# Three modulation slices summed on VectorE, and a longer pad ahead of the expert tiles, in a hybrid retention and mixture-of-experts layer

## The chip, the cores and the metric

One core of a Trainium2 chip runs the whole layer in one launch. The metric is the device time of an execution in microseconds; the time before is the median of three timed runs.

## The reference, cut to what matters

One layer over 2048 tokens of width 1024, in float32, with 256 context tokens and 16 experts. The modulation is one row vector, cut into six slices of 1024 numbers:

```python
mod = jax.nn.silu(c) @ w_ada[l] + b_ada[l]
sh1, sc1, g1, sh2, sc2, g2 = jnp.split(mod[:, None, :], 6, axis=-1)
h = modulate(x, sh1, sc1)                      # _ln(x) * (1 + sc1) + sh1
y = token_mixer(h @ w_in[l], ...)              # conv, retention, gates
x = layer_norm(DEEPNORM_ALPHA * x + g1 * y, ln1_g[l], ln1_b[l])
h = modulate(x, sh2, sc2)
x = layer_norm(DEEPNORM_ALPHA * x + g2 * expert_choice_ffn(h, ...), ln2_g[l], ln2_b[l])

def expert_choice_ffn(h, w_router, w_gate, w_up, w_down):   # 256 tokens for each of 16 experts
    he = jax.nn.silu(xe @ w_gate) * (xe @ w_up)
    ye = (he @ w_down) * gates                               # added back to the tokens' rows
```

## The kernel before

**Products.** A float32 product is made of three TensorE passes over split operands: `split` (L78) makes a high part on ScalarE and the remainder on VectorE, and `mm3` (L86) issues high x high, high x low and low x high, which are lines L87, L88 and L89 of the profile. Nearly all of PE's time is these three lines. The few products that are not split run on plain float32 tiles; each of them leaves two records in the trace.

**Stages.** The input stage multiplies the normalised tokens by `w_in`, whose columns come in groups of 512: U0, U1, K, V0, V1, Q, G0, G1, GA0, GA1, GB0, GB1. It goes over them twice, once for each half of the tokens (half 0, then half 1; four blocks of 256 tokens, called pids, in each), with one group's weight slabs (`sU`, `sG`, `sGA`, `sGB`, ...) on the chip at a time and the next group's being loaded and split. The transposed, normalised and modulated tokens of a pid are `hT`; `make_hT` makes them from row tiles `xt` of x (load, statistics on VectorE, `normalize` on ScalarE, transposes on PE at L281). The retention, the output projections, the mix with g1, sh2 and sc2 and the router follow, then 16 experts one after the other.

**What runs beside the projections.** `pump` steps through lists of generators at fixed places of the loop. In half 0 a pid's end also runs pieces of the depthwise convolution on VectorE (`conv_unit`, taps at L466), released by a one-column copy `anc` of the block's last result (L740). From group G0 of half 0 on each pid's end takes one step of `fillers2` (24 pids), and what is left is run out before half 1. `fillers2` holds `ada_rows` (L237): its first use makes g1 and sh2, its second sc2. A step is one of eight slices of 128 rows of `w_ada`: `ada_k` loads a piece `wa` of 128x1024 (two of them in a step of the first use, one in the second) into the ring `raw` (four buffers, shared with the weight slabs that wait to be split) and multiplies it by `crep`, the activated c spread over 32 columns, so that the results of 512 columns stand in one 32-row strip of a PSUM bank (L199). Behind the eighth step the bias `br` is loaded, added (L255), and one row of each strip stored to `d_mod` (L258), from where the mix reads it in a later stage. The fourth and last use of `ada_rows`, for g2, runs in the router stage and is not touched.

**Order.** Each engine runs its instructions in one row; a scheduler at build time sets it, within the limits that the pools (a tile waits for its slot to be free) and the explicit `issue_after` marks give. Loads and stores of this stage go through SyncE's queue. Tiles named with the tag `t4k` have three slots of 4 KB; `xt` uses them here.

**Experts.** The transposed tokens of an expert are `xeT` (high and low part, 8 slices of 256 tokens, two buffers of 16 KB), the hidden activations `heT` (the same shape, one buffer). Gate and up hold a block of the weight slab `sg` as stationary operand and move the 256 columns of `xeT`; down holds 128 tokens of `heT` as stationary operand and moves 512 columns of the slab `sd`. In the pool of this stage a tile `pad0` stands ahead of `heT`, and `pad1` ahead of `xeT`; they are never used and only set where the tiles behind them lie in a partition's memory. The slabs lie at 0 modulo 256 bytes throughout; `heT` lies at 128 and `xeT` at 160 modulo 256.

Of the kernel before, what the change touches and what calls it, by code (L numbers as in the profile page):

```python
# [9 lines left out]
F32 = mybir.dt.float32  # L10
# [5 lines left out]
ALU = mybir.AluOpType  # L16
# [4 lines left out]
P = 128  # L21
D = 1024
KD = 8
# [19 lines left out]
def body(ctx: ExitStack, tc: tile.TileContext, x, ctxt, cc, w_ada0, w_ada, b_row, b_col, w_in, conv_w, conv_b,  # L43
         conv_g, conv_bb, w_conv, lgf, lgb, gn_g, w_ret, w_out, ln1_g, ln1_b, w_router,
         w_gate, w_up, w_down, ln2_g, ln2_b, k_rope, k_pos, k_dif, k_sel, k_iota, k_bits, out):
    nc = tc.nc
    V, A, G, T = nc.vector, nc.scalar, nc.gpsimd, nc.tensor
# [7 lines left out]
    def dram(name, shape, dt=F32):  # L55
        return dr.tile(shape, dt, name=name, tag=name)
# [4 lines left out]
    def raw(name, shape):  # L61
        return wp.tile(shape, F32, name=name, tag="raw", bufs=4)
# [9 lines left out]
    def tr_ps(name="tr"):  # L72
        return pp.tile([P, 512], F32, name=name, tag="tr", bufs=2)

    def u_ps(name="u"):
        return pp.tile([P, 512], F32, name=name, tag="u", bufs=2)
# [31 lines left out]
    mhalf = const.tile([P, 8], F32, name="mhalf")  # L108
# [18 lines left out]
    d_mod = dram("d_mod", [8, 512])  # L127
# [36 lines left out]
    ip = inp.enter_context(tc.tile_pool(name="ip", bufs=1))  # L164
# [11 lines left out]
    sg = sm.tile([P, KD, 2], F32, name="sg", bufs=1)  # L176
# [3 lines left out]
    def rep_c(pool):  # L180
        crep = pool.tile([P, KD, 16, 2], F32, name="crep")
        made = V.tensor_copy(crep, sg[:, :, None, :].to_broadcast([P, KD, 16, 2]))
        return crep.rearrange("p k r c -> p k (r c)"), made

    crep, made = rep_c(ip)
# [4 lines left out]
    def ada_k(crep, c0, ps, k, halves=2, pre=None):  # L190
        for half in range(halves):
            if pre is not None:
                wt = pre[k // 4][:, k % 4]
            else:
                wt = raw(f"wa{c0}_{k}_{half}", [P, D])
                nc.sync.dma_start(wt, w_ada[c0 // D - 2 + half, k])
            for j in range(2):
                jj = half * 2 + j
                T.matmul(ps[32 * jj:32 * jj + 32, :], crep[:, k], wt[:, j * 512:(j + 1) * 512],  # L199
                         start=k == 0, stop=k == KD - 1)  # L200
                if pre is not None:
                    yield
        if pre is None:
            yield
# [32 lines left out]
    def ada_rows(crep, rnd, halves, tmp, pre=None):  # L237
        c0 = 2048 * (rnd + 1) if rnd < 2 else 5120
        n = 2 * halves

        def load_b():
            br = tmp("br")
            for j in range(n):
                nc.sync.dma_start(br[32 * j:32 * j + 32], bass.AP(tensor=b_row.tensor, offset=b_row.offset + c0 + 512 * j,
                                                                  ap=[[0, 32], [1, 512]]))
            return br

        ps = u_ps(f"ada{rnd + 1}")
        br = load_b() if pre is not None else None
        for k in range(KD):  # L250
            yield from ada_k(crep, c0, ps, k, halves, pre)
        mr = tmp("mr")
        if br is None:
            br = load_b()
        V.tensor_tensor(mr[:32 * n], ps[:32 * n], br[:32 * n], ALU.add)  # L255
        for j in range(n):
            r = c0 // 512 - 4 + j
            nc.sync.dma_start(d_mod[r:r + 1], mr[32 * j:32 * j + 1])  # L258
        yield
# [71 lines left out]
    fillers, fillers2, late, mids, outs = [], [], [], [], []  # L331
# [340 lines left out]
    for half in range(2):  # L672
        pairs = [half * 4 + i for i in range(4)]
        for gi, g in enumerate(GROUPS):
# [5 lines left out]
            for pi, pid in enumerate(plist):  # L680
# [30 lines left out]
                else:  # L711
                    pss = [mm_ps(), mm_ps()]
                    for k in range(KD):
                        for t in range(2):
                            lastmm = mm3(pss[t], hT(pid, k, t), slabs[k], k == 0, k == KD - 1)
                        if k == 3 and half == 1 and g == "GB1" and pi == 3:
                            with tc.issue_after(lastmm.ins):
                                prev, _ = ret_a(NT - 1, None)
# [26 lines left out]
            if g == "U1":  # L745
                fillers.append(conv_unit(list(range(0, 7)) if half == 0 else list(range(7, 16))))
            if half == 0 and g == "Q":
                fillers2.append(ada_rows(crep, 0, 2, t2k))
                fillers2.append(ada_rows(crep, 1, 1, t2k))
            if half == 0 and g == "GA1":  # L750
                make_hT(4, x, 8, 0)
            slabs = nslabs
# [141 lines left out]
    ep = moe.enter_context(tc.tile_pool(name="ep", bufs=1))  # L894
# [29 lines left out]
    same, low = ksel[:, 0], ksel[:, 1]  # L924
    wg2 = []
    for i, (tag, bufs) in enumerate((("heT", 1), ("xeT", 2))):
        V.memset(ep.tile([P, (24, 8)[i]], F32, name=f"pad{i}"), 0.0)
        wg2.append(ep.tile([P, 4, D], F32, name="wg2", tag=tag, bufs=bufs))
        nc.sync.dma_start(wg2[i], w_ada[3, i * 4:i * 4 + 4].rearrange("k p f -> p k f"))
    g2fill = [ada_rows(rep_c(ep)[0], 2, 1, lambda name: e4k(name, [P, 512]), wg2)]  # L930
    with tc.issue_after(pows[0].ins), tc.issue_after(exps[0].ins):
        first = [[gu_slabs(w[0], f2, True) for w in (w_gate, w_up)] for f2 in range(3)]
    segb = e2k("seg")
    seg = segb[:, :256]
    ps = tr_ps()
# [12 lines left out]
    for i in range(14, -1, -1):  # L948
        cnt = tk("cnt", 3, BF16, 2)
        for j in range(3):  # L950
# [3 lines left out]
                            op0=ALU.is_ge, op1=ALU.add, accum_out=cnt[:, j:j + 1])  # L954
# [47 lines left out]
    ps = tr_ps()  # L1002
# [132 lines left out]
    for e in range(NE):  # L1135
# [38 lines left out]
        for n in range(2):  # L1174
# [3 lines left out]
            for kk in range(4):  # L1178
                r = raw("rd", [P, 2, 512])
# [17 lines left out]
            if last:  # L1197
                for t in range(2):
# [4 lines left out]
                    for hf in range(2):  # L1203
                        z, c = zs[t], slice(hf * 512, (hf + 1) * 512)
                        V.scalar_tensor_tensor(z[:, c], z[:, c], mv[:, 0, 0:1], l2[0][:, c], op0=ALU.subtract, op1=ALU.mult)
                    for hf in range(2):
                        z, c = zs[t], slice(hf * 512, (hf + 1) * 512)
# [83 lines left out]
```

## Time and profile before

| what | value |
| --- | --- |
| median of the timed runs | 3068.63 us (3064.36 to 3070.91) |
| the profiled execution's own time | 3070.69 us |
| its span in the profile | 3068.9 us |
| PE (TensorE) busy | 2978.8 us, 97% of the span |
| PEld (weight loads, beside PE) | 2603.1 us, 85% |
| DVE (VectorE) | 2114.8 us, 69% |
| ACT (ScalarE) | 1158.3 us, 38% |
| POOL (GpSimd) | 361.2 us, 12% |

The durations that the profile gives for matmuls overlap: a matmul is in the array while the next one is already starting. How much a step takes from the clock is therefore read from the distance between two starts, not from its duration. The idle time in front of an instruction is given with what ended it.

### The profile page before, as it was taken

The numbers are of one execution on the slowest core, as the hardware profiler recorded it, in microseconds if no ns is written. First come the engines' busy times: TensorE is split into PE (matmuls) and PEld (weight loads), VectorE is DVE, ScalarE is ACT, GpSimd is POOL, SyncE is SP. The second block draws the span as 40 slices with busy tenths as digits, with TensorE's granted clock in tenths as the row PEclk, the third lists the DMA queues.
The fourth block names the chain that finished last, engine by engine and source line by source line (L and its number), as shares of the span: only waits on it lengthen the run. The fifth ranks groups of instructions, "written<-read, shape, count | busy, mean of one in ns | idle before, by whom it ended". The sixth has DMA issues, their size and how long they took to land. (4 is left out here: it accounts for less than half of the span.)

```text
span 3068.9 us, 47411 instructions
## 1 busy us (share of the span) xinstructions
PE 2978.8 (97%) x18089; PEld 2603.1 (85%) x18089; DVE 2114.8 (69%) x3898; ACT 1158.3 (38%) x2110; POOL 361.2 (12%) x325
## 2 busy tenths in 40 slices
PE   6999999999999999999999996999999999999998
PEld 5988877789888888888878883999999999999987
DVE  4366777442678986888867777566666666568886
ACT  4323122242231333544421112555555555544443
POOL 2100000000000000111101114010100000012331
PEclk9999999999999999999999997999999999999999
DMA  7334455332452334666764445667677667778875
GB/s 249 106 121 172 146 178 173 116 110 82 170 190 82 122 117 144 215 206 206 242 209 152 145 138 183 198 203 206 211 216 215 216 209 211 214 245 269 274 239 202
DMA packets 195044, 560.25 MB, mean 183 GB/s; under 512 B 29064, under 2 KB 44328, under 8 KB 194816
## 3 DMA queue, kind: packets, MB, share of 16 engines
q1 hardware_dynamic: 170272, 486.90, 47.8%
q0 software_dynamic: 18064, 64.62, 7.4%
q10 hardware_dynamic: 6480, 5.70, 0.6%
q8 instruction: 142, 2.33, 0.3%
q14 instruction: 86, 0.70, 0.1%
HBM read 429.24 MB, written 127.89 MB: 182 GB/s over the span
## 5 line engine op out<-in xcount | busy, mean ns | idle before, releaser
L87 PE MATMUL mm<-xeT,sg 128*128 128x256 f32 x2048 | 577.0, 282 | 0.0
L89 PE MATMUL mm<-xeT,sg 128*128 128x256 f32 x2048 | 575.6, 281 | 1.2 <-DVE sg L81 1.2
L88 PE MATMUL mm<-xeT,sg 128*128 128x256 f32 x2048 | 575.5, 281 | 0.0
L81 DVE TENSOR_TENSOR sg<-rg,sg 128x512 fp32r<-128x512 f32 x488 | 329.8, 690 | 249.2 <-ACT sg L80 244.5
L80 ACT ACTIVATE sg<-rg 128x512 fp32r<-128x512 f32 x512 | 313.5, 629 | 321.8 <-PE mm L89 222.6
L89 PEld LDWEIGHTS mm<-xeT,sg 128*128 128x128 f32 x2048 | 386.1, 189 | 1.4 <-DVE sg L81 1.4
L88 PEld LDWEIGHTS mm<-xeT,sg 128*128 128x128 f32 x2048 | 386.2, 189 | 0.7
L87 PEld LDWEIGHTS mm<-xeT,sg 128*128 128x128 f32 x2048 | 385.9, 189 | 0.7
L466 DVE SCALAR_TENSOR_TENSOR cacc<-yw,cvw,cacc 128x384 f32<-128x384 f32 (+1 forms) x600 | 376.8, 641 | 8.7
L81 DVE TENSOR_TENSOR sd<-rd,sd 128x512 fp32r<-128x512 f32 x256 | 172.6, 688 | 89.9 <-ACT sd L80 89.1
L80 ACT ACTIVATE sd<-rd 128x512 fp32r<-128x512 f32 x256 | 157.2, 629 | 135.3 <-PE mm L89 88.3
L88 PE MATMUL mm<-sd,heT 128*128 128x512 f32 x512 | 203.0, 397 | 3.7 <-DVE sd L81 3.7
L89 PE MATMUL mm<-sd,heT 128*128 128x512 f32 x512 | 203.1, 397 | 1.9 <-DVE heT L81 1.9
L87 PE MATMUL mm<-sd,heT 128*128 128x512 f32 x512 | 203.1, 397 | 1.4 <-ACT heT L80 1.4
L154 POOL TENSOR_TENSOR rs<-rs,mhalf 128x1 f32<-128x1 f32 (+1 forms) x50 | 37.6, 752 | 1294.1 <-DVE rs L153 1278.1
L87 PE MATMUL mm<-hT,sU 128*128 128x256 f32 x512 | 146.1, 288 | 4.4 <-ACT us L707 2.2
L88 PE MATMUL mm<-hT,sU 128*128 128x256 f32 x512 | 146.0, 286 | 0.0
L89 PE MATMUL mm<-hT,sU 128*128 128x256 f32 x512 | 145.1, 285 | 0.0
L147 POOL TENSOR_TENSOR rs<-rs,mhalf 128x1 f32<-128x1 f32 x58 | 86.6, 1493 | 365.9 <-DVE rs L146 365.7
L88 PEld LDWEIGHTS mm<-sd,heT 128*128 128x128 f32 x512 | 96.7, 189 | 27.4 <-DVE sd L81 5.4
L89 PEld LDWEIGHTS mm<-sd,heT 128*128 128x128 f32 x512 | 96.6, 189 | 25.9 <-DVE heT L81 3.1
L443 ACT ACTIVATE gs<-mm 128x512 f32<-128x512 f32 x96 | 54.9, 597 | 168.2 <-PE mm L89 133.0
(357 smaller groups left out, 7073.7 us busy)
## 6 DMA issues: line engine op xcount, KB each, us to landing
rg<-w_gate SPq DMA_DIRECT2D x128, 512.0 KB
rg<-w_up SPq DMA_DIRECT2D x128, 512.0 KB
rd<-w_down SPq DMA_DIRECT2D x128, 512.0 KB
wa<-w_ada SPq DMA_DIRECT2D x40, 512.0 KB
d_v<-vs SPq DMA_DIRECT2D x32, 512.0 KB
vsr<-d_v SPq DMA_DIRECT2D x32, 512.0 KB
xt<-x SPq DMA_DIRECT2D x16, 512.0 KB
rU<-w_in SPq DMA_DIRECT2D x16, 512.0 KB
```

Source lines behind the costliest of these rows:

```text
L80: A.activation(hi, src, AF.Copy)
L81: eng.tensor_tensor(lo, src, hi.bitcast(F32), ALU.subtract)
L87: T.matmul(ps, s[0], m[0], start=start, stop=False)
L88: T.matmul(ps, s[0], m[1], start=False, stop=False)
L89: return T.matmul(ps, s[1], m[0], start=False, stop=stop_)
L147: pows[0] = G.tensor_tensor(rs, rs, mhalf[:, :1], ALU.pow)
L154: G.tensor_tensor(rs[:, 0], rs[:, 0], mhalf[:, :heads], ALU.pow)
L443: A.activation(s, ps, AF.Sigmoid)
L466: V.scalar_tensor_tensor(acc[:, :n], y[:, tap:tap + n], cvw[:, cgp, tap:tap + 1], acc[:, :n], op0=ALU.mult, op1=ALU.add)
```

## The change

The edit has two parts. `ada_sums` takes the place of the two uses of `ada_rows` in the input stage. It makes one slice of 1024 columns: eight steps multiply a piece of `w_ada` by a per-partition number of the activated c and add it up in a tile `acc` on VectorE, and a ninth step adds up the 128 partitions with two matmuls against a tile of -0.5 of eight columns (`mhalf`), scales by -2 and adds the bias on VectorE, and stores. Three slices have 27 steps where there were 16, one for each of the 24 pids and three that are run out before half 1. `acc` uses the `t4k` slots of the row tiles. The second part lengthens `pad0` from 24 to 56 numbers, by 128 bytes, so `heT` stands at 0 modulo 256 bytes and `xeT` at 32; nothing else of the expert stage's order changes.

```diff
+    def ada_sums(c0, tmp):
+
+        acc = ip.tile([P, D], F32, name="acc", tag="t4k", bufs=3)
+        for k in range(KD):
+            wt = raw(f"wa{c0}_{k}", [P, D])
+            nc.sync.dma_start(wt, w_ada[c0 // D - 2, k])
+            if k == 0:
+                V.tensor_scalar(acc, wt, sg[:, k, 0:1], None, op0=ALU.mult)
+            else:
+                V.scalar_tensor_tensor(acc, wt, sg[:, k, 0:1], acc, op0=ALU.mult, op1=ALU.add)
+            yield
+        ps = u_ps(f"ada{c0}")
+        br = tmp("br")
+        mr = tmp("mr")
+        for j in range(2):
+            c = slice(32 * j, 32 * j + 8)
+            nc.sync.dma_start(br[c], bass.AP(tensor=b_row.tensor, offset=b_row.offset + c0 + 512 * j, ap=[[0, 8], [1, 512]]))
+            T.matmul(ps[c], mhalf, acc[:, j * 512:(j + 1) * 512], start=True, stop=True)
+        for j in range(2):
+            c = slice(32 * j, 32 * j + 8)
+            V.scalar_tensor_tensor(mr[c], ps[c], -2.0, br[c], op0=ALU.mult, op1=ALU.add)
+            r = c0 // 512 - 4 + j
+            nc.sync.dma_start(d_mod[r:r + 1], mr[32 * j:32 * j + 1])
+        yield
...
             if half == 0 and g == "Q":
-                fillers2.append(ada_rows(crep, 0, 2, t2k))
-                fillers2.append(ada_rows(crep, 1, 1, t2k))
+                fillers2.extend(ada_sums(c0, t2k) for c0 in (2048, 3072, 4096))
...
     for i, (tag, bufs) in enumerate((("heT", 1), ("xeT", 2))):
-        V.memset(ep.tile([P, (24, 8)[i]], F32, name=f"pad{i}"), 0.0)
+        V.memset(ep.tile([P, (56, 8)[i]], F32, name=f"pad{i}"), 0.0)
```

Behind the new function all lines stand 25 (from L747 on 24) lower: the taps are L491 there, the transposes of x L306, the loads of x L289.

**In group G0 of half 0, PE's row before**, from the end of the first pid to the start of the second:

```order
1987 L88 MATMUL mm_3773<-sG031_3662,hT0_3_303 128x512
1988 L89 MATMUL mm_3773<-sG031_3662,hT0_3_303 128x512
1990 L160 MATMUL tr_3830<-ident_73,q_3753 128x128 x4
1991 L199 MATMUL ada1_3856<-wa2048_0_0_3857,crep_283 32x512 x2
1992 L199 MATMUL ada1_3856<-wa2048_0_1_3861,crep_283 32x512 x2
1993 L87 MATMUL mm_3865<-sG000_3635,hT1_0_324 128x512
```

The two L199 lines are one step; there are eight such steps at pids' ends, and eight with one L199 line.

**PE's row after, in GA0, where the first of the three new steps stands:**

```order
2393 L88 MATMUL mm_4556<-sGA031_4448,hT0_3_303 128x512
2394 L89 MATMUL mm_4556<-sGA031_4448,hT0_3_303 128x512
2395 L278 MATMUL ada2048_4621<-acc_3856,mhalf_88 8x512 x2
2396 L87 MATMUL mm_4632<-sGA000_4421,hT1_0_324 128x512
2397 L88 MATMUL mm_4632<-sGA000_4421,hT1_0_324 128x512
```

Ahead of it no pid's end has a step on PE any more; the second stands at the end of a pid in GB0, the third at the end of half 0.

**DVE's row after, around the end of group Q**, where the first two sums stand among taps, splits and the state updates of the retention (`acc` the running sum, `cacc` the convolution's, `q` the rotated queries):

```order
349 L81 TENSOR_TENSOR vs_3325<-mm_3275,vs_3325 128x512
350 L268 TENSOR_SCALAR acc_3856<-wa2048_0_3857,sg_280 128x1024
351 L461 SCALAR_TENSOR_TENSOR S_3333<-S_3219,dect_285,u_3332 128x256
...
360 L81 TENSOR_TENSOR sG031_3662<-rG03_3657,sG031_3662 128x512
361 L491 SCALAR_TENSOR_TENSOR cacc_3270<-yw_3268,cvw_274,cacc_3270 128x512
362 L270 SCALAR_TENSOR_TENSOR acc_3856<-wa2048_1_3928,sg_280,acc_3856 128x1024
363 L491 SCALAR_TENSOR_TENSOR cacc_3270<-yw_3268,cvw_274,cacc_3270 128x512
364 L377 TENSOR_TENSOR ra_3430<-mm_3377,cs_3428 128x512
```

Before, this stretch has no such rows; the scheduler places the sums one at a time, some ahead of the pid whose end they belong to.

**At the end of half 0, SP's row before** (`gs` the evicted gates, `rU` the weights of half 1's first group):

```order
252 L264 DMA xt_5950<-x 128x1024
253 L264 DMA xt_6016<-x 128x1024
261 L244 DMA br_5438<-b_row 32x512 x2
262 L258 DMA d_mod_258<-mr_5437 1x512 x2
280 L447 DMA d_gb7_194<-gs_5941 128x512
281 L264 DMA xt_6018<-x 128x1024
```

**and after:**

```order
267 L266 DMA wa4096_7_5922<-w_ada 128x1024
279 L472 DMA d_gb7_194<-gs_5913 128x512
280 L277 DMA br_5926<-b_row 8x512 x2
281 L289 DMA xt_6008<-x 128x1024
282 L283 DMA d_mod_258<-mr_5927 1x512 x2
283 L289 DMA xt_6010<-x 128x1024
```

The row tile that was loaded 28 rows ahead of the last gate store (xt_6016, now xt_6008) stands behind that store, and the second one behind the last store to `d_mod`. On PE the third new step stands directly ahead of the first transposes of half 1:

```order
3147 L89 MATMUL mm_5861<-sGB131_5485,hT3_3_954 128x512
3148 L278 MATMUL ada4096_5925<-acc_5492,mhalf_88 8x512 x2
3149 L306 MATMUL tr_5964<-ident_73,xt_5940 128x128
3150 L306 MATMUL tr_5964<-ident_73,xt_5942 128x128
3157 L87 MATMUL mm_6072<-hT4_0_5186,sU000_5827 128x256
```

In the kernel before the same transposes follow the last L89 of GB1 directly.

## Rows read from the trace of the kernel before

**Rows 1.** The page, busy time by engine:

```profile
PE 2978.8 (97%) x18089; PEld 2603.1 (85%) x18089; DVE 2114.8 (69%) x3898; ACT 1158.3 (38%) x2110; POOL 361.2 (12%) x325
```

**Rows 2.** Busy time by stretch: length, PE, PEld, DVE, ACT, POOL, clock, DMA:

```profile
380.00:650.00 270.00, 270.00 (x1242) 209.80 (x1241) 162.50 (x318) 71.42 (x129) 8.22 (x14) 1.00 0.44 148
430.00:480.00 50.00, 50.00 (x248) 38.45 (x246) 41.33 (x91) 18.69 (x36) 4.83 (x8) 1.00 0.55 189
2250.00:2400.00 150.00, 150.00 (x1078) 141.14 (x1077) 93.47 (x138) 80.13 (x134) 10.33 (x8) 1.00 0.71 211
2960.00:3000.00 40.00, 32.85 (x176) 26.81 (x175) 32.01 (x51) 10.82 (x19) 16.48 (x11) 0.96 0.69 218
```

**Rows 3.** PE's waits, 320 to 700 us: releaser, total, times, longest:

```profile
PE tr L281 <- ACT xt L269: 1.0, 2, 0.5
```

**Rows 4.** Groups of instructions on PE, shapes apart: busy, mean ns of one:

```profile
L199 PE MATMUL ada<-wa,crep 128*32 128x512 f32 x96 | 16.9, 605 | 0.0
...
L88 PE MATMUL mm<-sGA,hT 128*128 128x512 f32 x256 | 99.7, 389 | 0.0
...
L88 PE MATMUL mm<-sd,heT 128*128 128x512 f32 x512 | 203.0, 397 | 3.7 <-DVE sd L81 3.7
...
L88 PE MATMUL mm<-xeT,sg 128*128 128x256 f32 x2048 | 575.5, 281 | 0.0
```

**Rows 5.** PE's timeline around two modulation steps: start, duration:

```profile
390.83 1.06 PE L199 MATMUL ada<-wa,crep 128*32 128x512 f32 x8
391.83 0.50 PE L87 MATMUL mm<-sG,hT 128*128 128x512 f32 x1
392.17 0.39 PE L88 MATMUL mm<-sG,hT 128*128 128x512 f32 x1
...
501.73 0.39 PE L89 MATMUL mm<-sGA,hT 128*128 128x512 f32 x1
502.05 1.05 PE L199 MATMUL ada<-wa,crep 128*32 128x512 f32 x4
503.03 0.50 PE L87 MATMUL mm<-sGA,hT 128*128 128x512 f32 x1
503.37 0.39 PE L88 MATMUL mm<-sGA,hT 128*128 128x512 f32 x1
```

**Rows 6.** PE's timeline, first row of an undisturbed stretch of GA0:

```profile
491.08 0.39 PE L87 MATMUL mm<-sGA,hT 128*128 128x512 f32 x1
```

**Rows 7.** Groups of instructions on DVE, shapes apart: busy, mean ns of one:

```profile
L1193 DVE SCALAR_TENSOR_TENSOR ye<-mm,gate,g2r 128x512 f32<-128x512 f32 x64 | 45.3, 745 | 12.8 <-PE mm L89 12.8
...
L824 DVE SCALAR_TENSOR_TENSOR h<-xl,mv,sc2r 128x1024 f32<-128x1024 f32 x16 | 20.4, 1276 | 0.0
...
L255 DVE TENSOR_TENSOR mr<-ada,br 64x512 f32<-64x512 f32 x2 | 1.4, 676 | 0.0
...
L775 DVE TENSOR_SCALAR sc2r<-sc2r 128x1024 f32<-128x1024 f32 x1 | 0.7, 694 | 1.4 <-DMA sc2r<-d_mod 1.4
```

**Rows 8.** PE's timeline, ends of undisturbed stretches of U, gate/up and down:

```profile
668.59 1.03 PE L281 MATMUL tr<-ident,xt 128*128 128x128 f32 x8
...
674.31 0.28 PE L88 MATMUL mm<-hT,sU 128*128 128x256 f32 x1
...
679.34 0.28 PE L88 MATMUL mm<-hT,sU 128*128 128x256 f32 x1
...
2084.53 0.28 PE L89 MATMUL mm<-xeT,sg 128*128 128x256 f32 x1
...
2090.58 0.28 PE L89 MATMUL mm<-xeT,sg 128*128 128x256 f32 x1
...
2119.53 0.39 PE L87 MATMUL mm<-sd,heT 128*128 128x512 f32 x1
...
2130.02 0.40 PE L87 MATMUL mm<-sd,heT 128*128 128x512 f32 x1
```

**Rows 9.** PE's timeline, down of the last experts, idle before in brackets:

```profile
2967.10 0.50 PE L89 MATMUL mm<-sd,heT 128*128 128x512 f32 x1 [1.45 <-DVE heT L81]
...
2979.72 0.53 PE L88 MATMUL mm<-sd,heT 128*128 128x512 f32 x1 [2.15 <-DVE sd L81]
```

## The prediction

> **What bounds the kernel now.** I read the busy time of the engines first: TensorE is busy for 2978.8 of the span, 97% [rows 1]. Then the table of busy time by stretch, at the two places that the change touches. From 380 to 650 us, where the three slices g1, sh2 and sc2 of the modulation are made beside the gate projections, PE is busy for all 270.00 us at full clock, and VectorE for 162.50; from 2250 to 2400, among the experts, PE again for all 150.00 [rows 2]. The list of PE's waits confirms it for the input stage: from 320 to 700 us PE waits 1.0 us in all, twice, both times for a row tile of x at the start of half 1 [rows 3]. So in both places the time is the sum of PE's steps, start to start, and a step that leaves PE shortens the kernel by its whole length so long as nothing that feeds PE falls behind. Only the last experts differ: from 2960 to 3000 PE is busy for 32.85 of 40 us [rows 2].
>
> The busy time of one matmul overlaps with its neighbours (390 ns busy, a new one every 227), so I price PE steps by starts.
>
> **1. Modulation steps that leave PE.** Before, 16 steps of L199 stand between the projections, 8 with four column strips (96 records in all, two for each of 48 fp32 matmuls, [rows 4]). What one costs: the projection matmul before it starts at 501.73, the second one after it at 503.37, which is 1.64 us [rows 5]. Two steps of the undisturbed pace are 2 x 0.2266 = 0.453: from 491.08 [rows 6] to 501.73 [rows 5] lie 47 steps, 10.65/47 = 226.6 ns. So a two-strip step costs 1.18 us. A four-strip step is no dearer: from its start to the second projection matmul behind it go 390.83 to 392.17, 1.34 us, against 502.05 to 503.37, 1.32 [rows 5]. The term is 16 x 1.18 = **-18.9 us**. (Only the one four-strip row beside transposes stands for eight, so I allow 1.1 for these: -18.2.)
>
> **2. What comes back on PE.** Three steps of two fp32 matmuls, 8 columns of weights instead of 32, 512 columns moved: the shape of the two-strip step. 3 x 1.18 = **+3.5 us**. Bounds: 3 x 0.45 = 1.4, if two matmuls cost as two of the pace, and 3.5.
>
> **3. VectorE.** It gets 21 SCALAR_TENSOR_TENSOR and 3 TENSOR_SCALAR over 128x1024, and 6 evictions of 8x512 in place of 2. Prices: the same operation at that size takes 1276 ns at L824, TENSOR_SCALAR 694 ns at L775; an STT from PSUM over 512 columns 745 ns at L1193; the two removed additions some 676 ns each [rows 7]. 21 x 1.276 + 3 x 0.694 + 6 x 0.745 - 2 x 0.676 = 26.8 + 2.1 + 4.5 - 1.4 = 32.0 us. Spread evenly over the 270 us, VectorE goes from 162.5 to 194.5, 72%: it fits. Its tightest piece is 430 to 480, 41.33 of 50 [rows 2]; an even share of the 32 us adds 32 x 50/270 = 5.9, 47.3 of 50. It still fits, but with the free time gone the evictions of G1 come late, and PE has two banks to run ahead. If the sums come at twice the even density there, 41.3 + 11.8 = 53.1: 3.1 over, and one or two more such pieces could follow. The cost lies between 0 and 10 us; I take **+2**, nearest to the even case, because the order puts one sum at a time between taps and evictions. Each sum also frees a slot of the raw ring, and the loads of the next weight slabs queue behind the loads of wa on SP: that was so before, with PE as the reader, and the 24 loads are the same.
>
> **4. Start of half 1.** The accumulator is a third user of the x tiles' slots. In the new order the load of xt_6008 stands on SP behind all wa loads and the last br loads, and waits until the last of the three new matmuls has read its sum; xt_6010 stands behind the store of mr, which waits for VectorE. Before, two x tiles of that place were loaded well ahead, and PE waited 1.0 us for them [rows 3]. In the new order of PE some 100 matmuls, nearly all of the U projection at 119.8 ns [rows 8], stand between that matmul and the first transpose of xt_6008: 12 us for a load, four-odd VectorE steps and an activation. Probably nearly enough: **+2**, between 0 and 6. The readers of the three slices come after half 1 and wait for nothing here; the U bank that the old step held is merely free earlier.
>
> **5. Down's stationary operand moves from 128 to 0 of 256 bytes.** Down is the only 512-column group whose heT stands at 128, and the only one whose matmuls read 397 ns; the others (row of sGA, both operands at 0) read 389 [rows 4]. By starts, 2119.53 to 2130.02 are 45 steps, 233.1 ns [rows 8], against 226.6: 6.5 ns each. There are 3 x 512 = 1536 of them [rows 4], so 10.0 us; in the last two experts PE waits for weight slabs in just these matmuls (1.45 and 2.15 us for heT and sd, [rows 9]), so I keep 14/16: **-8.7 us**. Bounds: 0, if the address is not what makes them long, and -8 x 1.536 = -12.3, by busy time.
>
> A rule speaks against this term. The Trainium skill, page "SBUF — State Buffer", section "Specifications (TRN2)", states 16-byte cachelines and a penalty for each crossing to a new line, and its "Operand start alignment" asks only for a multiple of the element size; 0, 32, 128 and 160 are all multiples of 16, so by it no start would matter. The 6.5 ns between two groups of one shape here disagree, unless they come from something else in down. By the rule term 5 would be 0.
>
> **6. Gate's and up's tokens move from 160 to 32 of 256 bytes.** 6144 matmuls [rows 4], so each ns is 6.1 us. No matmul of before has an operand at 32. With tokens at 160 the pace is 2084.53 to 2090.58 in 51 steps, 118.6 ns; the U projection, same shape with both operands at 0, takes 674.31 to 679.34 in 42 steps, 119.8 [rows 8]. So 160 pays nothing against 0, and 32, like 160 an odd multiple of 32, is nearest to it: **0**. If it behaved as 0 does, +1.2 x 6.144 = +7.4 us; if it paid what heT pays at 128, +6.5 x 6.144 = +39.9. Downward, half of a 512-column step is 113.3 ns, -5.3 x 6.144 = -32.6, which no 256-column row reaches; halfway would be -16.
>
> **Sum.** -18.9 + 3.5 + 2 + 2 - 8.7 + 0 = -20.1 us. The profiled execution took 3070.69 us, so 3050.6 on its scale; it lies 2.1 above the median of 3068.63, so the median of after should be 3068.63 - 20.1 = 3048.5, **3049 us**.
>
> **The rivals.** (a) The pads change nothing. For it: down differs from the projections also in that its slabs arrive just in time, and no row shows an address. Against: these waits are counted apart, and PE in 2250 to 2400 has none [rows 2]. Time: 3048.5 + 8.7 = 3057. This is what the cited rule gives. (b) VectorE becomes the bound of G0 and G1 and PE waits in place of the steps that it lost: 10 us where I took 2, 3057; with late x tiles (6 where I took 2) 3061. For it: 41.33 of 50; against: 162.5 of 270. (c) The other side: tokens at 32 pay as the stationary operand at 128 does. Place: L87 to L89 of gate and up, PE-bound through all experts; price 6.5 ns x 6144 = 40 us; 3048.5 + 39.9 = 3088, slower. It makes the kernel slower from 20.1/6.144 = 3.3 ns a matmul on. For it: one misplaced operand is seen to cost 6.5 ns at 397 against 389; against: 160 cost nothing. (d) Tokens at 32 behave as 0: 3056. (e) Tokens at 32 are better than at 160: halfway to the floor, 3033. That the change doesn't do what it says would be that the tiles stand elsewhere: heT was at 128 behind a pad of 24 floats, and 32 floats more are 128 bytes, so this needs no chance.
>
> **How the numbers follow.** The forecast (3043 to 3054) 0.49; (a) 0.12; (b) 0.12; (c) 0.11; (d) 0.08; (e) 0.08. About 0.2%, 6.1 us, is what a measurement of this kernel can tell from no change: faster is below 3062.5, slower above 3074.8. All of the forecast, (a), (d) and (e) are faster; (b) mostly, and in part with (a) or (d) on top within 0.2%; (c) is slower, its milder sizes within. Faster 0.78, same 0.11, slower 0.11. The range leaves out (c) and the low half of (e), and takes in (a), (b) and (d): 3034 to 3063.
>
> **What would show it.** Step 1: no L199 rows between 390 and 590, and the first transposes of half 1 some 13 us earlier than at 668.59 [rows 8]; if they come less early, PE's waits for evictions in 390 to 650 show step 3. Step 4: waits of the x transposes above 1.0 us. Step 5: sd,heT at 389 instead of 397, pace near 226.6. Step 6: xeT,sg at 281 and the pace at 118.6. A down row still at 397 makes (a) right; a gate row of 285 or more makes (c) or (d) right.

## The result and the profile after

The changed kernel takes 3041.86 us (median of 4 runs, 3037.94 to 3044.82), the kernel before 3069.77 in the same comparison: ratio 0.9911, 95% interval 0.9895 to 0.9926, so 27.9 us less where 20.1 were forecast. The sign, the range (3034 to 3063) and the mechanism of two of the three large terms held; the third, put at nothing, gave over a third of the gain. So the time fell just below the band of 3043 to 3054 that the forecast gave itself, on the side of rival (e), 3033, which had a chance of 0.08.

The page and the stretches of the profile after, busy time by engine, as [rows 1, 2]:

```profile
PE 2948.3 (97%) x18005; PEld 2596.3 (85%) x18005; DVE 2141.8 (70%) x3926; ACT 1161.0 (38%) x2110; POOL 361.5 (12%) x325
...
380.00:650.00 270.00, 270.00 (x1233) 222.01 (x1232) 195.75 (x360) 79.69 (x139) 12.02 (x18) 1.00 0.46 155
2250.00:2400.00 150.00, 150.00 (x1057) 140.34 (x1056) 95.20 (x142) 80.47 (x135) 10.82 (x8) 1.00 0.71 214
```

PE still has no free time in either place, so the time went out of its steps, not out of waits. VectorE between 380 and 650 rose from 162.50 to 195.75 us, 33 where 32.0 were added up. PE's waits from 320 to 700 us, as [rows 3]:

```profile
PE tr L306 <- ACT xt L294: 1.8, 2, 1.1
```

No wait for an eviction appears, only the x tiles of half 1, 0.8 us more than before. One of the three new steps in PE's timeline, as [rows 5]:

```profile
484.46 0.39 PE L89 MATMUL mm<-sGA,hT 128*128 128x512 f32 x1
484.78 1.03 PE L278 MATMUL ada<-acc,mhalf 128*8 128x512 f32 x4
485.74 0.50 PE L87 MATMUL mm<-sGA,hT 128*128 128x512 f32 x1
486.07 0.39 PE L88 MATMUL mm<-sGA,hT 128*128 128x512 f32 x1
```

From 484.46 to 486.07 are 1.61 us, 1.16 more than two plain steps: eight columns of weights cost within 0.02 us as much as 32 (1.18 in the prediction). The groups of PE and of VectorE with their mean duration, as [rows 4, 7]:

```profile
L278 PE MATMUL ada<-acc,mhalf 128*8 128x512 f32 x12 | 3.1, 594 | 0.0
...
L88 PE MATMUL mm<-sGA,hT 128*128 128x512 f32 x256 | 99.7, 389 | 0.0
...
L88 PE MATMUL mm<-sd,heT 128*128 128x512 f32 x512 | 201.4, 393 | 2.7 <-DVE sd L81 2.7
...
L88 PE MATMUL mm<-xeT,sg 128*128 128x256 f32 x2048 | 571.8, 279 | 0.0
...
L270 DVE SCALAR_TENSOR_TENSOR acc<-wa,sg,acc 128x1024 f32<-128x1024 f32 x21 | 26.9, 1279 | 7.5 <-DMA wa<-w_ada 7.3
...
L268 DVE TENSOR_SCALAR acc<-wa,sg 128x1024 f32<-128x1024 f32 x3 | 2.3, 751 | 0.8 <-DMA wa<-w_ada 0.8
...
L281 DVE SCALAR_TENSOR_TENSOR mr<-ada,br 8x512 f32<-8x512 f32 x6 | 4.1, 680 | 10.3 <-DMA br<-b_row 10.2
```

Of PE, the 96 L199 records of [rows 4] are gone and 12 of L278 stand for them. Down went from 397 to 393 and gate and up from 281 to 279 ns. The VectorE prices are within a tenth of those in [rows 7] (1279 for 1276, 751 for 694, 680 for 745 ns), and these rows add up to 26.9 + 2.3 + 4.1 - 1.4 = 31.9 us. The last row shows a new wait that nobody pays for: VectorE stands 10.2 us, in two pieces, until a bias load lands.

By the distance of starts, as [rows 6, 8], in the same expert of the timeline:

```profile
2052.54 0.28 PE L87 MATMUL mm<-xeT,sg 128*128 128x256 f32 x1
...
2074.82 0.28 PE L89 MATMUL mm<-xeT,sg 128*128 128x256 f32 x1
...
2103.70 0.39 PE L88 MATMUL mm<-sd,heT 128*128 128x512 f32 x1
...
2113.90 0.39 PE L88 MATMUL mm<-sd,heT 128*128 128x512 f32 x1
```

Gate and up: 191 steps in 22.28 us, 116.7 ns, where 118.6 stood before. Down: 45 steps in 10.20 us, 226.7, where 233.1 stood. Over all pairs of neighbouring rows of a group (a distance over 160 ns, or 300 for down, counted as a wait and left out) the paces are 118.47 before and 116.76 after for gate and up, 232.79 and 227.15 for down.

To see where the 28.6 us between the two profiled executions (3070.69 and 3042.10) went, I read the start of the first row of each stage from the timelines and took the length of the pieces, in us. The columns to the right are the experiments below.

| piece | before | after | after_again | e1_pads | e2_sums | e3_twice |
| --- | --- | --- | --- | --- | --- | --- |
| start to group Q of half 0 | 331.0 | 334.3 | 331.1 | 332.9 | 334.8 | 333.0 |
| Q of half 0 to U of half 1 | 338.3 | 322.7 | 322.7 | 338.4 | 322.6 | 322.6 |
| U of half 1 to Q of half 1 | 244.4 | 245.0 | 244.8 | 244.4 | 244.8 | 244.4 |
| Q of half 1 to the first expert | 1012.0 | 1010.6 | 1009.1 | 1012.4 | 1012.4 | 1013.7 |
| first expert to down of the 15th | 1029.8 | 1011.3 | 1014.3 | 1011.7 | 1030.6 | 1012.9 |
| from there to the last down matmul | 101.8 | 104.9 | 102.8 | 99.4 | 102.2 | 105.7 |

The second row is the modulation, the fifth the pad. The first holds nothing that the change touches; in the fourth only the weight tiles for g2 stand elsewhere, since they use the slots of heT and xeT.

### The profile page after: what moved, and what is told of

The parts are those of the page before. It is cut to its first block, busy times and chain, and to the rows that moved or that the text cites. A ratio compares the mean times of both kernels' runs of the same rounds, so it can differ in the third digit from the quotient of the medians.

```text
span 3040.3 us, 47284 instructions
## 1 busy us (share of the span) xinstructions
PE 2948.3 (97%) x18005; PEld 2596.3 (85%) x18005; DVE 2141.8 (70%) x3926; ACT 1161.0 (38%) x2110; POOL 361.5 (12%) x325
## 5 line engine op out<-in xcount | busy, mean ns | idle before, releaser
L89 PE MATMUL mm<-xeT,sg 128*128 128x256 f32 x2048 | 572.3, 280 | 1.2 <-DVE sg L81 1.2
L89 PEld LDWEIGHTS mm<-xeT,sg 128*128 128x128 f32 x2048 | 385.0, 188 | 1.4 <-DVE sg L81 1.4
L491 DVE SCALAR_TENSOR_TENSOR cacc<-yw,cvw,cacc 128x384 f32<-128x384 f32 (+1 forms) x600 | 376.7, 641 | 8.0
L89 PE MATMUL mm<-sd,heT 128*128 128x512 f32 x512 | 201.4, 393 | 1.8 <-DVE heT L81 1.8
L89 PE MATMUL mm<-hT,sU 128*128 128x256 f32 x512 | 147.2, 289 | 0.0
L1245 POOL DMA_INDIRECT d_acc<-ye,idx x30 | 50.5, 1684 | 570.9 <-DVE ye L1217 470.8
L87 PEld LDWEIGHTS mm<-sd,heT 128*128 128x128 f32 x512 | 97.3, 190 | 24.4 <-ACT heT L80 4.6
```

The source lines that it names most:

```text
L87: T.matmul(ps, s[0], m[0], start=start, stop=False)
L89: return T.matmul(ps, s[1], m[0], start=False, stop=stop_)
L491: V.scalar_tensor_tensor(acc[:, :n], y[:, tap:tap + n], cvw[:, cgp, tap:tap + 1], acc[:, :n], op0=ALU.mult, op1=ALU.add)
L1245: G.indirect_dma_start(out=d_acc, out_offset=bass.IndirectOffsetOnAxis(ap=idx[:, g:g + 1], axis=0), in_=yes[t], in_offset=None, compute_op ...
```

## The experiments

### The pad alone: e1_pads

```diff
-        V.memset(ep.tile([P, (24, 8)[i]], F32, name=f"pad{i}"), 0.0)
+        V.memset(ep.tile([P, (56, 8)[i]], F32, name=f"pad{i}"), 0.0)
```

> The kernel before with only the longer pad: heT at 0, xeT at 32 of 256 bytes, modulation slices on TensorE as before. Theory A (the two parts are independent and the pad is worth what the pace of the two trace groups shows): down at about 227 ns a step instead of 232.8, gate and up at about 116.8 instead of 118.5, so 1536 x 5.7 + 6144 x 1.7 = 19.2 us less, some 3 of them lost again in the last two experts, where slabs arrive late: 16 us faster than before, ratio 0.9948. Rival B (the lower gate and up pace of the changed kernel comes from something that the modulation part moved, such as when loads fall): gate and up stay at 118.5, down goes to 227: 6 to 8 us faster.

3054.95 us (5 runs), ratio 0.9946, interval 0.9933 to 0.9960: theory A's 16 us. The pace of gate and up is 116.68 ns, of down 227.12, and the input stage is that of before (338.4 in the table). Its two rows among PE's groups:

```profile
L88 PE MATMUL mm<-xeT,sg 128*128 128x256 f32 x2048 | 571.9, 279 | 0.0
...
L88 PE MATMUL mm<-sd,heT 128*128 128x512 f32 x512 | 200.5, 392 | 3.8 <-DVE sd L81 3.8
```

So 32 floats of unused memory are worth some 16 us, without any help from the sums. Rival B is out. The 3 us that the expectation took to be lost in the last two experts were not lost in this profile (99.4 in the table's last row, 101.8 before).

### The sums alone: e2_sums

```diff
-        V.memset(ep.tile([P, (56, 8)[i]], F32, name=f"pad{i}"), 0.0)
+        V.memset(ep.tile([P, (24, 8)[i]], F32, name=f"pad{i}"), 0.0)
```

> The changed kernel with the old pad of 24 floats: only the modulation slices move to VectorE. Theory A: the input stage from G0 to the U projection of half 1 is 15 us shorter, less about 1 at the start of half 1, and the experts run at 232.8 and 118.5 ns as before: 14 us faster than before, ratio 0.9954. Rival B (part of the gain among the experts belongs to this part): the expert paces are below 232.8 and 118.5 here, and it is 17 us or more faster. Rival C (the 3 us that the changed kernel was late at the second load of the first modulation are caused by the change, not by the run): the start of group Q of half 0 is again some 3 us later than in the kernel before, and the gain is 11 us.

3059.31 us (5 runs), ratio 0.9955, interval 0.9941 to 0.9968. By the medians that is 12.0 us less than before, by the ratio 13.8, so the time alone does not tell theory A's 14 from rival C's 11. The paces are back at 118.59 and 233.07 ns, and the rows among PE's groups are those of before:

```profile
L88 PE MATMUL mm<-xeT,sg 128*128 128x256 f32 x2048 | 575.6, 281 | 0.0
...
L88 PE MATMUL mm<-sd,heT 128*128 128x512 f32 x512 | 203.1, 397 | 3.9 <-DVE sd L81 3.9
```

Rival B is out. Rival C's sign did appear (334.8 in the table's first row), but e1_pads, whose input stage is that of the kernel before, shows 332.9, and a second profile of the changed kernel 331.1: the first loads scatter from one execution to the next. So nothing shows this delay to be the change's, and the piece that the sums do touch is 15.7 us shorter, as theory A had it. The two parts add: 0.9946 x 0.9955 = 0.9901, against 0.9911 together, within the intervals.

### Room on VectorE: e3_twice

```diff
                 V.scalar_tensor_tensor(acc, wt, sg[:, k, 0:1], acc, op0=ALU.mult, op1=ALU.add)
+            V.scalar_tensor_tensor(acc, wt, 0.0, acc, op0=ALU.mult, op1=ALU.add)
             yield
```

> The changed kernel with each of the 24 steps of the sums followed by one more SCALAR_TENSOR_TENSOR of 128x1024 that adds the piece times 0.0, so the sum is the same and VectorE has 24 x 1.28 = 31 us more in the input stage. Theory A (VectorE has room from 380 to 650: 196 of 270 us busy): VectorE goes to 227 of 270, and the time stays within 3 us of the changed kernel's 3042, with PE's waits from 320 to 700 below 5 us. Rival (VectorE is close to its limit there, and the sums as they stand already use up what the scheduler can hide): PE waits for evictions in G0 and G1, and the time rises by 10 to 31 us.

3045.22 us (4 runs), ratio 0.9912, interval 0.9897 to 0.9927. The stretches and PE's waits from 320 to 700 us:

```profile
380.00:650.00 270.00, 270.00 (x1233) 222.13 (x1232) 216.36 (x380) 79.49 (x138) 11.62 (x18) 1.00 0.46 155
430.00:480.00 50.00, 50.00 (x237) 41.62 (x236) 46.22 (x96) 19.74 (x38) 4.39 (x8) 1.00 0.39 139
...
PE tr L307 <- ACT xt L295: 1.4, 2, 0.7
```

VectorE is busy for 216 of 270 us, 20.6 more than in the changed kernel where the expectation had 31 (over the whole execution its busy time rose by 23.4), and the piece from Q to U is 322.6 us as it was. The time is 3.2 us above the 3042 that the expectation named, just beyond its 3, but against the kernel before in the same comparison the ratio is that of the changed kernel (0.9912 for 0.9911). The evictions were not pushed late enough for PE to see it. Rival (b) of the prediction is out with a margin: the sums done nearly twice left PE's stretch as long as it was.

### Where the tokens stand: x0, x64, x96, x128, x192, x224

The second pad alone was changed (heT stays at 0), to 64, 16, 24, 32, 48 and 56 numbers in place of 8; 160 is the kernel before and 32 the changed one.

```diff
-        V.memset(ep.tile([P, (56, 8)[i]], F32, name=f"pad{i}"), 0.0)
+        V.memset(ep.tile([P, (56, 64)[i]], F32, name=f"pad{i}"), 0.0)
```

> The changed kernel with the second pad at 64 numbers: heT stays at 0, xeT moves from 32 to 0 of 256 bytes. So far gate and up run at 118.5 ns with xeT at 160 and 116.8 at 32, and the U projection, the same shape with its moving operand at 0, at 119.9. Theory A (what counts is where the moving operand starts, and 0 is as dear as in the U projection): 119.9 ns, 3.1 x 6.144 = 19 us slower than the changed kernel, some 3061. Rival B (only the half of the 256 bytes counts, 0 to 127 against 128 to 255; the U projection is slower for another reason): 116.8 ns and 3042.

> The changed kernel with xeT at 96 of 256 bytes (second pad 24 numbers), heT at 0. Theory A (some start off 0 is cheaper, whatever the half): 96 lies as far from a multiple of 128 as 32 does, so 116.8 ns and 3042. Rival B (only the half counts): 116.8 as well. A third possibility, that each step of 64 bytes adds (32 cheap, 160 dearer, 96 between): about 117.6 ns, 3047.

> The changed kernel with xeT at 128 of 256 bytes (second pad 32 numbers), heT at 0. Theory A (a start at a multiple of 128 is dear for the moving operand): about 120 to 121.5 ns, 3061 to 3070. Rival B (only the half counts): 118.5 as at 160, 3052. Rival C, that the moving operand pays at 128 what the stationary one does (5.7 ns over its best): 122.5 ns, 3077.

> The changed kernel with xeT at 64 of 256 bytes, heT at 0. Measured for gate and up so far: 120.0 ns at 0, 116.8 at 32, 120.0 at 96, 119.5 at 128, 118.5 at 160. Theory A (32 is the best place of each 128 bytes, so a start pays by its distance from 32): about 118.4 ns, 10 us slower than the changed kernel, 3052. Rival B (32 of each 64 bytes would be best, which 96 already contradicts, or 0 and 64 behave alike): 120.0 ns, 3061.

> The changed kernel with xeT at 192 of 256 bytes, heT at 0. Theory A (a start pays by its distance from 32 in each 128 bytes, and the upper half a little more): about 119 to 120 ns, 3056 to 3062. Rival B (0, 64, 128 and 192 behave alike): 120.0 ns, 3061.

> The changed kernel with xeT at 224 of 256 bytes, heT at 0. Theory A (32 is the best place of each 128 bytes): as at 96, 120.0 ns or a little more, 3061. Rival B (a place next to 0 of the following 256 bytes is as good as 32, because the two parts of a tile lie 1024 bytes apart and only the crossing counts): 117 ns, 3043.

| xeT modulo 256 bytes | 0 | 32 | 64 | 96 | 128 | 160 | 192 | 224 |
| --- | --- | --- | --- | --- | --- | --- | --- | --- |
| gate and up, ns a step | 119.96 | 116.76 | 117.45 | 120.00 | 119.53 | 118.47 | 115.75 | 118.32 |
| one execution, us | 3060.86 | 3042.10 | 3044.38 | 3062.89 | 3055.60 | (3070.69) | 3042.01 | 3047.33 |

(The time under 160 is that of the kernel before, with heT at 128 and the old modulation. Each time is a single execution, and those of the changed kernel alone lie between 3037.94 and 3050.19, so the paces tell the starts apart and the times only the large steps. The tiles that lie behind xeT in the pool move with the second pad too, but of the matmuls' two operands only xeT moves; down, whose operands stay, kept to 226.9 to 227.1 ns in all six runs.) The row of x0 among PE's groups, and the ends of the same stretch of 191 steps as above:

```profile
L88 PE MATMUL mm<-xeT,sg 128*128 128x256 f32 x2048 | 580.0, 283 | 0.0
...
2058.82 0.28 PE L87 MATMUL mm<-xeT,sg 128*128 128x256 f32 x1
...
2081.73 0.28 PE L89 MATMUL mm<-xeT,sg 128*128 128x256 f32 x1
```

22.91/191 = 119.9 ns, within 0.2 of the U projection's 119.8, whose moving operand also starts at 0 [rows 8]. x0 met theory A, time included (3061). The other theories of these runs fell: the half of the 256 bytes does not decide (0 and 96 are dear, 192 is cheap), nor does the distance from 32 in each 128 bytes (32 and 160 lie alike and differ by 1.7 ns, 192 lies as far from it as 128 and is 3.8 cheaper), nor is every multiple of 64 alike. At 128 the pace came near theory A's 120, at a lower time than it gave. So the start changes the price, but the eight means follow no rule that I could find.

The start does not set the price alone either. The transposes of the next expert's tokens cut an expert's 384 gate and up matmuls into two halves of 192. At 0, 96 and 224 every half runs at one pace (119.9 to 120.0, 120.0, 118.3 ns). At the other starts there are two paces, and a half keeps to one of them almost throughout; counted over the 32 halves of one profile each:

| xeT modulo 256 bytes | 32 | 64 | 128 | 160 | 192 |
| --- | --- | --- | --- | --- | --- |
| the commoner pace, ns (halves) | 116.7 (30) | 117.8 (29) | 120.0 (21) | 118.7 (27) | 117.8 (17) |
| the other, ns (halves) | 117.8 (2) | 113.4 (2), and one mixed | 118.6 (11) | 117.4 (5) | 113.4 (15) |

Both paces stand in one expert of x192_timed, ahead of the transposes and behind them:

```profile
2324.43 0.28 PE L87 MATMUL mm<-xeT,sg 128*128 128x256 f32 x1
...
2346.92 0.28 PE L89 MATMUL mm<-xeT,sg 128*128 128x256 f32 x1
2347.04 1.91 PE L160 MATMUL tr<-ident,xe 128*128 128x128 f32 x16
...
2349.03 0.28 PE L89 MATMUL mm<-xeT,sg 128*128 128x256 f32 x1
...
2370.46 0.28 PE L89 MATMUL mm<-xeT,sg 128*128 128x256 f32 x1
```

191 steps in 22.49 us are 117.8 ns, 189 steps in 21.43 us are 113.4, the half of a 512-column step that the prediction took as the floor. The two stretches, with the granted clock in the last but two column:

```profile
2324.40:2346.90 22.50, 22.50 (x192) 22.47 (x191) 13.66 (x21) 12.02 (x21) 3.48 (x2) 1.00 0.83 233
2349.00:2370.40 21.40, 21.40 (x191) 21.40 (x190) 13.93 (x22) 12.49 (x21) 1.84 (x2) 1.00 0.70 225
```

PE is busy throughout and the clock is full in both, so neither waits nor the clock make the difference. What picks the pace of a half stays open, and the means under 64, 128, 160 and 192 depend on how often each is picked.

### Down's stationary operand at 32: h32

```diff
-        V.memset(ep.tile([P, (56, 8)[i]], F32, name=f"pad{i}"), 0.0)
+        if i:
+            V.memset(ep.tile([P, 64], F32, name=f"pad{i}"), 0.0)
```

> The changed kernel with heT at 32 and xeT at 32 of 256 bytes (no first pad, second pad 64 numbers). Down's stationary operand at 32. Theory A (the stationary operand is dear when it starts in the upper half or off a multiple of 256): if any offset costs, about 233 ns, 1536 x 5.9 = 9 us slower, 3051. Rival B (only the upper half costs): 227 ns, 3042. Gate and up stay at 116.8 in both.

3051.43 us in one execution; down at 233.27 ns, gate and up at 116.83. Down's row among PE's groups:

```profile
L88 PE MATMUL mm<-sd,heT 128*128 128x512 f32 x512 | 203.5, 397 | 3.9 <-DVE sd L81 3.9
```

397 ns again, as at 128 [rows 4], and 9 us more than the changed kernel, as theory A said. The second pad is longer here by what the first one lost, so xeT and all behind it stay where they were and heT alone has moved. For down's stationary operand both starts off 0 that were tried cost about 6 ns a matmul; for gate's and up's moving one 32 is cheaper than 0 in the same memory. The other operand of each, the slab, stood at 0 in every run, so how two starts act together is not shown.

### The changed kernel again, and tokens at 192, timed: after_again, x192_timed

> The changed kernel once more, unaltered, beside the next one on one chip. Both theories: ratio to the kernel before about 0.991, gate and up at 116.8 ns, down at 227. The start of group Q of half 0, ahead of everything that the change touches, should scatter by a few us between profiles (341.6 before, 343 to 345 in five others), which says that the first loads and not the change set it.

> The changed kernel with xeT at 192 of 256 bytes, timed. Its gate and up read 115.75 ns in one profile against 116.76 with xeT at 32. Theory A (the pace decides, since PE is the bound through 14 of 16 experts): 1.0 x 6144 x 14/16 = 5.4 us faster than the changed kernel, some 3036. Rival B (the experts' loads and VectorE's splits are by now so close behind PE that a faster pace only waits more): the same 3042 within 2 us.

The changed kernel took 3043.79 us (5 runs, 3038.08 to 3050.19; ratio 0.9920, interval 0.9906 to 0.9933), the one with xeT at 192 3036.16 (4 runs, 3035.68 to 3039.72; ratio 0.9890, interval 0.9875 to 0.9905). That is the best time of all, 7.6 us under the changed kernel beside it, and theory A's 3036 came out; the intervals lie side by side (0.9905 and 0.9906), so 192 is barely clear of 32. The profiles do not show theory A's 5.4 us, though: the piece from the first expert to down of the 15th takes 1010.0 us in x192 and 1011.6 in x192_timed, and 1011.3 to 1014.3 in the table's four profiles with xeT at 32. The distances that the paces leave out as waits exceed the pace by 5.1 and 5.7 us in all there, against 2.3 to 4.6 in these four, so a part of the faster pace is waited away, as rival B has it, and the rest of the 7.6 us is not traced. The group rows of both read 279 ns for xeT,sg; by starts the means are 116.70 and 115.89. Group Q of half 0 started at 331.1 us in after_again, where the expectation counts from a point 10.5 us ahead of the span's start (341.6): as in the kernel before, so its delay in the first profile was the run's.

## Why the prediction was right, and where it was off

**Modulation steps and their return (steps 1 and 2), -15.4 forecast.** Measured: the piece from Q of half 0 to U of half 1 went from 338.3 to 322.7 us, -15.7, and to the same 322.6 or 322.7 in the eleven other profiles with the sums. Pricing by starts was right to 0.3 us: the 16 steps at 1.18, the three new ones at 1.16. Adding up busy time would have given 16.9 - 3.1 = 13.8.

**VectorE (step 3), +2 forecast, between 0 and 10.** Measured 0. The amount was right (31.9 us by its rows for 32.0), and e3_twice shows that even nearly twice the sums leave PE alone. No eviction came late enough for PE to wait; whether the two banks covered it or the order kept the evictions early, no run tells apart.

**Start of half 1 (step 4), +2 forecast.** Measured 0.4 to 0.6 us on the piece behind it in the two profiles of the changed kernel, 0.0 in e3_twice; PE's waits there rose from 1.0 to 1.8 us. The terms of steps 3 and 4, 4 us together, came to less than 1. The 12 us of U matmuls covered the late load almost whole.

**Down (step 5), -8.7 forecast, 6.5 ns a matmul.** Measured 5.64 ns x 1536 = 8.7 us in all, some 7.6 of it ahead of the last two experts. The reading was right: the address makes down longer, which e2_sums shows by putting heT back to 128 and h32 by moving it alone to 32, both with 397 ns and some 233 by starts. Of the 6.5 ns it accounts for 5.6; the rest, 227.15 against 226.6 for the gates, is something else in down. The stretch in [rows 8] was a little slower than the mean of all down rows.

**Gate and up (step 6), 0 forecast.** This is the step that was off: measured -1.71 ns x 6144 = -10.5 us. I had two rows, 118.6 at 160 and 119.8 at 0, and took 32 to be like 160 since both are odd multiples of 32. The two rows already said that the start matters for the moving operand too, by 1.2 ns; that two unlike starts differ is a reason to expect a third value and not the nearer of the two. The rival (e), better than at 160, had a chance of 0.08 and should have had as much as (c) and (d) together, since nothing in the two rows said which way. The sign that the step had set for itself, 281 ns and 118.6 by starts, did not appear (279 and 116.7). And the trace before held a third row that I did not read, the second half of its sixth expert, with xeT at 160 as well:

```profile
2305.77 0.28 PE L89 MATMUL mm<-xeT,sg 128*128 128x256 f32 x1
...
2327.94 0.28 PE L89 MATMUL mm<-xeT,sg 128*128 128x256 f32 x1
```

These 189 steps take 22.17 us, 117.3 ns each, as four other halves do to within 0.2 ns: one start had two prices, so a single stretch could not give the price of 160, let alone that of 32. Rival (c), 40 us dearer, is out: the dearest of eight starts costs 1.5 ns more than 160, not 6.5.

**Rival (a), that the pads change nothing,** is out: all eight starts are multiples of 32, and gate and up take from 115.75 to 120.0 ns in the mean. The prediction's reading of the Trainium skill's page "SBUF — State Buffer", that with the 16-byte cachelines of "Specifications (TRN2)" no such start would matter, does not agree with these runs. The Trainium skill's section "Operand start alignment" on that page speaks of which starts are legal, not of speed, so the runs do not contradict it.

**The sum.** -15.7 + 0.6 in the input stage, -18.5 from the first expert to the 15th's down (15 x 384 x 1.71 + 14 x 96 x 5.64 = 17.4 by the paces), and then +3.1 in the last two experts, +3.2 by the first loads and -1.4 in the untouched middle, both of which other profiles show with other signs: -28.7. That the total came within 8 us of the forecast is in part luck: steps 3 and 4 were put 3 us too dear, step 6 was short by 10.5, and the last two experts gave some back.

**What was given back at the end.** In the last two experts PE waits for down's inputs, before as after, and by their paces alone these two should be 2.4 us shorter. The stretches around these waits, with the granted clock in the last but two column, after and then before:

```profile
2923.00:2963.00 40.00, 32.51 (x152) 26.20 (x150) 34.94 (x57) 11.34 (x21) 17.88 (x12) 0.91 0.55 185
...
3002.00:3030.00 28.00, 25.13 (x107) 19.86 (x105) 21.90 (x37) 3.75 (x7) 9.63 (x6) 0.94 0.14 56
```

```profile
2955.00:2995.00 40.00, 32.85 (x159) 25.95 (x158) 34.21 (x55) 10.33 (x18) 16.57 (x12) 0.96 0.60 192
...
3033.00:3058.00 25.00, 24.00 (x106) 18.70 (x104) 20.17 (x33) 2.92 (x6) 5.57 (x6) 1.00 0.11 45
```

PE's waits for heT, sd and sg are somewhat longer, 9.5 us in all from 2923 to 3030 against 7.9 from 2955 to 3058 before, and the clock stands lower after: 0.91 for 0.96 and 0.94 for 1.00. In the timeline the lower clock is seen directly behind two waits of 2.18 and 1.43 us:

```profile
2934.38 0.50 PE L87 MATMUL mm<-sd,heT 128*128 128x512 f32 x1 [2.18 <-ACT heT L80]
...
2936.54 0.79 PE L89 MATMUL mm<-sd,heT 128*128 128x512 f32 x1 [1.43 <-DVE heT L81]
2937.14 0.63 PE L87 MATMUL mm<-sd,heT 128*128 128x512 f32 x1
2937.56 0.63 PE L88 MATMUL mm<-sd,heT 128*128 128x512 f32 x1
```

The distance of starts is 0.42 us where it was 0.227: the 1.2 GHz level in place of 2.4, until 2939.27. Across the two stretches 40 x 0.05 + 28 x 0.06 = 3.7 us of full clock are missing, which with the 1.6 us of longer waits is near the 3.1 + 2.4 = 5.5 us to be explained; how much of the 3.7 fell into waits, where it costs nothing, was not worked out. Whether it comes differs between profiles (the piece took 102.8 us in after_again and 99.4 in e1_pads), so it was not traced further.

## What to carry to other kernels

Compare the start-to-start pace of groups of one shape: a difference of 2 to 6 ns a matmul that no wait explains is worth that times thousands of matmuls, and an unused pad is a cheap way to test whether an operand's place in memory causes it. Test several starts, for the stationary and the moving operand apart, since 0 was good for the one and dear for the other here and no rule was found. Read more than one stretch of a group, since one start can have two paces. And a small product with one row of weights that is repeated over many columns can leave a saturated TensorE for a VectorE with free time at its start-to-start price, less that of the few matmuls that add up the partitions; here that held with VectorE busy for up to 216 of 270 us, and nothing fuller was tried.

## What the runs showed of the hardware that I had not expected

- The start of the moving operand changes the pace of 256-column matmuls, between 115.75 and 120.0 ns in the mean over eight starts 32 bytes apart, without an order in the starts; 0 and 96 are the dearest. The stationary operand of down costs 5.6 to 6.2 ns more at 32 and at 128 than at 0.
- At 32, 64, 128, 160 and 192 the same start gives two paces, at 192 for instance 113.4 and 117.8 ns with the granted clock at 1.00 in both, each kept for nearly all of the 192 matmuls of a half expert. What picks one of them stays open.
- Two fp32 matmuls of 8 columns take as long as two of 32 (1.16 and 1.18 us by starts), and nearly as long as four of 32 at once (1.20 us: in the trace before, a step between projections takes 1.65 from 402.62 to 404.27, less 0.45 for two plain steps).
